# Where single-token state space steps, a gate's last products and the layer's input are placed in a hybrid layer

## The chip, the cores and the metric

One core of a Trainium2 chip runs the whole kernel. The metric is the device time of one execution in microseconds (us); a version is run several times and the median is shown. Inputs and outputs are float32 arrays in the chip's memory.

## The reference

One layer of a decoder is computed for 1024 prompt tokens and for 8 single tokens ("samples", one per sequence, each with a state of its own from earlier). Cut to what matters here:

```python
proj = rmsnorm(x, norm1_w) @ w_in                 # q, f, i, g, z, xbc, dt
xbc = silu(causal_dwconv(xbc, buf, conv_w, b))    # x (16 heads of 64), B and C (2 groups of 128)
# state space group: for a sample token, one step
S_new = exp(A * dt) * S + (x * dt) outer B
y = S_new @ C + D * x
y = rmsnorm(y * silu(z)) per group of 512 channels
# HGRN2 group: 8 heads with a matrix state, own gate and norm
x = x + concat([o_hgrn, y]) @ w_out               # the layer's input x is added here
x = x + (silu(conv(gate)) * val) @ w_down         # gate, val = rmsnorm(x) @ w_up
y = rmsnorm(x) * final_w
```

For the prompt tokens the state space part is computed in 8 chunks of 128 tokens. All new states are outputs too.

## The kernel before

The activations are kept with channels on the 128 partitions and tokens along the free dimension: 1032 columns, 1024 of the prompt (`T`) and 8 of the samples (`T:NT`). Every large product is made of three matmuls on rounded parts (high by high, high by low, low by high), so the tensor engine has much to do.

The work before `w_down` is a list of **jobs**, each with one weight tile. A job of the input projection is 72 matmuls (three column blocks of 344). The order is x0 to x3 (first group's x), x9 and x11 (second group's B and C), x4 to x7 (second group's x), z0 to z3 (first gate), the first head's f, q, v, sg, then z4 to z7, then the other heads' jobs f1 to sg7. The first group's B and C tiles (j = 8 and 10) are made ahead of the list. Then come the jobs of the output projection `o{r0}.{m}`: o8.0, o8.2, o12.0, o12.2, o8.4, o8.6, o12.4, o12.6, and then o0 and o4 in two halves; rows 8 to 15 are the state space part, 0 to 7 the heads. A job of o8 sets two tiles of the sum (`A.copy`, L1038), the later ones add to them (L1040).

A **stream** runs beside jobs: `drive(stream, weight, name)` issues a stretch of the stream and then so many matmuls of jobs in proportion. `ssd(0)` (first group, 8 chunks) runs beside x9 to x7, `ssd(1)` beside z0 to the first head's q, and `head(h)` beside later jobs; `head(7)`, the last, runs beside o8.0 to o12.2. `ssd_front` builds a chunk's decays (`csb`, L530, L531, L546) and transposes x (`xp`, L541); `ssd_back` makes its output and the next state (`yo`, `st`, `yd`, L563 to L582).

`tick()` is called at each job matmul; `after(n, work)` runs `work` n ticks later, and `spread(pieces, n)` runs a generator one piece at a time, n ticks apart. Code that is issued earlier has priority. Only the tensor engine keeps the written order (`manual_schedule`). For the other engines and the DMA queue on SP the framework's scheduler makes an order when the program is built: an instruction that it holds to be ready may come ahead of earlier code. That order is then fixed, and each queue runs in it and waits at its head. `fetch` ties a load behind the last weight load issued (`issue_after`).

**The parts that the change touches:**
- `decode_bc(g)` (L606) transposes the samples' columns of B and C, copies them (`bcr`, L611) and writes them to memory (`bc_d`, L612). It is the first thing in the stream `ssd(g)`, so for group 0 it stands behind x3.
- `ssm_decode(g, i)` (L614) is the single step of x tile i for all 8 samples, in two halves of four. A half loads `Bb`, `Cb` and the state `Sd` (L623 to L626), scales the state on ScalarE (L627, four instructions), forms the new state on VectorE (L628, L629), stores it (L630), multiplies it by C on GpSimd (L631) and sums on VectorE (L632). The result goes into the samples' columns of the x tile (L633). `ddb` (dt and decay) is loaded at L499. Buffers: four for `Bb` and `Cb` together (tag `d`), two for `Sd` (tag `ld`). For group 0 the steps are issued at the start of x5, x7, z0 and z1; for group 1 at z4 to z7.
- `tail()` in `ssm_gate(g)` (L679) makes the four normalized products of a group (L683, 128x1032 each) and stores them (L684), all four where the norm of the last column block is ready, some 36 (group 0) or 50 (group 1) ticks into the job behind the gate.
- `residual_load(m)` (L756) loads 128 columns of the layer's input into two `xs` tiles (tag `d` as well) and an `xd`; `residual` transposes them (L774, L778) and adds them to the sum (L769), in two pieces 8 ticks apart. It is done for tiles m and m+1 in each of the four jobs of o8. `mix_load(r0)` loads four tiles of the mixers' output for the jobs of `r0` and splits them into high (ScalarE, L998) and low parts (VectorE, L999).

```python
    with tc.manual_schedule(engines={mybir.EngineType.PE}):
        finish("x3")
        drive(ssd(0), 45.5, "x7")
        drive(ssd(1), 45.5, "v0")
        finish("z7")
        for h in range(H):
            drive(head(h, heads[h]), 32.0 if h else 35.0, f"sg{h + 1}" if h < H - 1 else "o12.2")
        finish("o12.6")
```

Of the kernel before, what the change touches and what calls it, by code (L numbers as in the profile page):

```python
# [12 lines left out]
ALU = mybir.AluOpType  # L13
# [37 lines left out]
def hybrid_layer(  # L51
# [9 lines left out]
    V, A, G, PE, SP = nc.vector, nc.scalar, nc.gpsimd, nc.tensor, nc.sync  # L61
# [9 lines left out]
    def nm(s):  # L71
        cnt[0] += 1
        return f"{s}_{cnt[0]}"
# [142 lines left out]
    def after(n, work):  # L216

        later.append([n, work])
# [8 lines left out]
    def spread(pieces, n, then=None):  # L227

        def go():
            if next(pieces, 0) is None:  # L230
                after(n, go)
            elif then is not None:
                then()
        go()
# [115 lines left out]
    def xbc_close(j, ext):  # L350
# [6 lines left out]
        A.activation(acc[:, T:NT], acc[:, T + 3:T + 32:4], AF.Silu)  # L357
        return acc

    def xbc_job(j, put):  # L360
        ext = []
        def begin():
            ext.append(xbc_open())
            if j in (5, 7):
                ssm_decode(0, (5, 7).index(j))

        in_job(f"x{j}", OFF_X + j * P, lambda c, cs, ps: xbc_evict(j, ext[0], c, cs, ps), begin=begin, end=lambda: put(xbc_close(j, ext[0])))

# [65 lines left out]
    d_bc = const.tile([P, 8], F32, name="d_bc")  # L434
# [165 lines left out]
    def d4(t):  # L600
        return t.rearrange("p (b n) -> p b n", n=P)
# [4 lines left out]
    def decode_bc(g):  # L606
        bcps = bank("bc", "nx")
        for i, src in enumerate((BT[g], CT[g])):
            PE.transpose(bcps[:ND, i * P:(i + 1) * P], src[:, T:NT], ident)
        bcr = small.tile([ND, 2 * P], F32, tag="bcr", bufs=1, name=nm("bcr"))  # L610
        V.tensor_copy(bcr, bcps[:ND, :2 * P])  # L611
        SP.dma_start(bc_d[2 * g:2 * g + 2].rearrange("i b n -> b i n"), bcr.rearrange("b (i n) -> b i n", n=P))  # L612

    def ssm_decode(g, i):  # L614
        j = g * 4 + i
        xdd = small.tile([P, 2, ND], F32, tag="xdd", name=nm("xdd"))
        xdec = Xg[g][i][:, T:NT]
        V.tensor_tensor(xdd[:, 0, :], xdec, ddb[:, 0, j, :], op=ALU.mult)
        for b0 in (0, 4):
            bs = slice(b0, b0 + 4)  # L620
            Bb, Cb = tl("d", "Bb")[:, :512], tl("d", "Cb")[:, :512]
            for t_, r in ((Bb, 2 * g), (Cb, 2 * g + 1)):
                fetch(t_, bc_d[r, bs].rearrange("b n -> (b n)").unsqueeze(0).to_broadcast([P, 512]))  # L623
            Sd = tl("ld", "Sd")
            fetch(d4(Sd), state_ssm[0, bs, 2 * j:2 * j + 2].rearrange("b h p n -> (h p) b n"))
            for b in range(4):  # L626
                A.activation(d4(Sd)[:, b, :], d4(Sd)[:, b, :], AF.Copy, scale=ddb[:, 1, j, b0 + b:b0 + b + 1])  # L627
            V.tensor_tensor(d4(Bb), d4(Bb), cb(xdd[:, 0, bs]), op=ALU.mult)  # L628
            V.tensor_tensor(Sd, Sd, Bb, op=ALU.add)  # L629
            SP.dma_start(ssm_sample[0, bs, 2 * j:2 * j + 2].rearrange("b h p n -> (h p) b n"), d4(Sd))  # L630
            G.tensor_tensor(Cb, Sd, Cb, op=ALU.mult)  # L631
            V.tensor_reduce(xdd[:, 1, bs], d4(Cb), axis=mybir.AxisListType.X, op=ALU.add)  # L632
        V.scalar_tensor_tensor(xdec, xdec, d_bc[:, j:j + 1], xdd[:, 1, :], op0=ALU.mult, op1=ALU.add)  # L633

    def rstd_of(dst, tmp, ps, n):

# [5 lines left out]
    def ssm_gate(g):  # L642
        acc = []

        def z_job(i):
            j = g * 4 + i

            def begin():
                if i == 0:
                    acc.append(tl("g", "gacc"))  # L650
                if g:
                    ssm_decode(1, i)
                elif i < 2:
                    ssm_decode(0, i + 2)

            def evict(c, cs, ps):
                Y = Xg[g][i][:, cs]
                sz = tl("z", "sz")[:, :CH]
                A.activation(sz, ps, AF.Silu)
                V.tensor_tensor(Y, Y, sz, op=ALU.mult)  # L660
                if i == 0:
                    A.activation(acc[0][:, cs], Y, AF.Square)
                else:
                    A.activation(sz, Y, AF.Square)
                    (V if g or i == 3 else G).tensor_tensor(acc[0][:, cs], acc[0][:, cs], sz, op=ALU.add)
                if i == 3:
                    after(36 + 14 * g, lambda: rstd(c))
            in_job(f"z{j}", OFF_Z + j * P, evict, begin=begin)

        def rstd(c):  # L670
            cs = chunks[c]
            ps = bank("ms", "nx")
            mm(ps[:, :CH], ones, acc[0][:, cs])
            rstd_of(acc[0][:, cs], tl("z", "nt")[:, :CH], ps[:, :CH], 512)

            if c == NCH - 1:
                tail()

        def tail():  # L679
            for i in range(4):  # L680
                j = g * 4 + i
                Y = Xg[g][i][:, :NT]
                V.scalar_tensor_tensor(Y, Y, col("sn", j), acc[0][:, :NT], op0=ALU.mult, op1=ALU.mult)  # L683
                SP.dma_start(mix_d[8 + j], Y)  # L684

        for i in range(4):
            z_job(i)
# [13 lines left out]

    def ssd(g):
        parts = {}
        decode_bc(g)
        yield 6.5
        ssd_front(g, 0, parts)
        for c in range(1, NC):
            yield 2.5
            ssd_front(g, c, parts)
            yield 2.5  # L710
            ssd_back(parts, c - 1)
        yield 3.0
        ssd_back(parts, NC - 1)
        yield 1.0
        ssm_state_out(g)
# [40 lines left out]
    def residual_load(m):  # L756
        ms = slice(m * P, (m + 1) * P)
        xs = [tl("d", "xs")[:, :512] for _ in range(2)]
        xd = small.tile([ND, P], F32, tag="xd", name=nm("xd"))
        for i in range(2):  # L760
            fetch(xs[i].rearrange("p (i m) -> p i m", m=P),
                  x_prompt[0, i * 512:(i + 1) * 512, ms].rearrange("(i p) m -> p i m", p=P))
        fetch(xd, x_sample[:, 0, ms])
        return xs, xd
# [20 lines left out]
    xh = [[None] * KT for _ in range(2)]  # L785
# [226 lines left out]
    x1_d = dram.tile([KT, P, NT], F32, name="x1_d")  # L1012
    rst = tl("g", "n2r")

    def out_job(r0, m, halves=(0, 1), last=False):
        def load():
            w = wload(w_out[0, r0 * P:(r0 + 4) * P, m * P:(m + 2) * P], 4, 2 * P)
            return w, [residual_load(m + i) for i in range(2)] if r0 == 8 else None

        def run(loads):  # L1020
            w, res = loads
            if r0 not in mixes:
                mixes[r0] = mix_load(r0)
            hi, lo = mixes[r0]
            if res:
                for hf in range(2):
                    xpair[hf][m // 2] = tl("big", "x1")[:, :NT].rearrange("p (i t) -> p i t", i=2)
                    for i in range(2):
                        xh[hf][m + i] = xpair[hf][m // 2][:, i, :]
            for i in range(2):  # L1030
                for hf in halves:
                    for c in range(2):
                        cs, ts_ = slice(c * QW, (c + 1) * QW), slice((2 * hf + c) * QW, (2 * hf + c + 1) * QW)
                        ps = psmm.tile([P, 512], F32, tag="mm", name=nm("mm"))[:, :QW]
                        yield from steps(w, i * P, (i + 1) * P, hi, lo, ts_, ps)
                        x_ = xh[hf][m + i][:, cs]
                        if res:
                            A.copy(x_, ps)  # L1038
                        else:
                            V.tensor_tensor(x_, x_, ps, op=ALU.add)  # L1040
                        if last:
                            final(m + i, x_, ts_)
                        yield True
                if res:
                    spread(residual([xh[hf][m + i] for hf in range(2)], *res[i]), 8)
        job(f"o{r0}.{m}" + (f".{halves[0]}" if len(halves) == 1 else ""), load, run)

    def final(m, x_, ts_):
# [30 lines left out]
    for hf in range(2):  # L1079
        for r0 in (0, 4):  # L1080
            for m in range(0, KT, 2):
                out_job(r0, m, (hf,), r0 == 4)

    with tc.manual_schedule(engines={mybir.EngineType.PE}):
        finish("x3")
        drive(ssd(0), 45.5, "x7")
# [5 lines that stand above are left out]
        for r0 in (0, 4):  # L1092
            mixes[r0] = mix_load(r0)
# [307 lines left out]
    for c in (3, 0, 1, 2):  # L1401
# [4 lines left out]
        for t0 in range(cs.start, cs.stop, P):  # L1406
# [11 lines left out]
            for i in range(2):  # L1418
# [4 lines left out]
                else:  # L1423
                    V.scalar_tensor_tensor(ot[i][:n], tb[i][:n, :], ss[:n, 3:4], fw[:n, ds],  # L1424
                                           op0=ALU.mult, op1=ALU.mult)
# [31 lines left out]
```

## Time and profile before

| | |
|---|---|
| median of 3 runs | 1781.82 us (1781.15 to 1788.02) |
| the profiled execution's own time | 1782.61 us |
| its span, first to last instruction | 1780.9 us |
| TensorE matmul busy | 1725.4 us, 97% of the span |
| VectorE, ScalarE, GpSimd busy | 63%, 46%, 23% |
| DMA | 182.34 MB, mean 102 GB/s |

PE is the tensor engine, DVE is VectorE, ACT is ScalarE, POOL is GpSimd, SP the engine whose queue issues nearly all DMAs. A row of instructions has line, engine, operation, output and inputs. "Idle before" is the time in which the engine stood still ahead of an instruction, with what ended that. In a table of waits the three numbers are the sum in us, how often, and the longest. A granted clock of 1.00 is 2.4 GHz on the tensor engine, 0.50 is 1.2 GHz.

### The profile page before, as it was taken

The numbers are of one execution on the slowest core, as the hardware profiler recorded it, in microseconds if no ns is written. First come the engines' busy times: TensorE is split into PE (matmuls) and PEld (weight loads), VectorE is DVE, ScalarE is ACT, GpSimd is POOL, SyncE is SP. The second block draws the span as 40 slices with busy tenths as digits, with TensorE's granted clock in tenths as the row PEclk, the third lists the DMA queues.
The fourth block names the chain that finished last, engine by engine and source line by source line (L and its number), as shares of the span: only waits on it lengthen the run. The fifth ranks groups of instructions, "written<-read, shape, count | busy, mean of one in ns | idle before, by whom it ended". The sixth has DMA issues, their size and how long they took to land. (4 is left out here: it accounts for less than half of the span.)

```text
span 1780.9 us, 38506 instructions
## 1 busy us (share of the span) xinstructions
PE 1725.4 (97%) x16143; PEld 1675.6 (94%) x16143; DVE 1119.3 (63%) x2011; ACT 817.5 (46%) x1464; POOL 405.3 (23%) x415
## 2 busy tenths in 40 slices
PE   7999899999999999999999978999999999999998
PEld 6998799999999999999899978999999999999997
DVE  6667966575564565458645768666666666445545
ACT  7677688455554454545333435334333344111114
POOL 2113331220110111011000364554445542000001
PEclk9999999999999999999999998999999999999999
DMA  4144634642221222234334432222222225422212
GB/s 154 39 126 126 189 106 132 184 137 98 87 66 51 86 73 78 58 109 155 101 108 133 135 90 72 72 72 78 82 91 72 72 84 203 152 81 90 97 61 96
DMA packets 218019, 182.34 MB, mean 102 GB/s; under 512 B 13388, under 2 KB 195158, under 8 KB 217830
## 3 DMA queue, kind: packets, MB, share of 16 engines
q1 hardware_dynamic: 217558, 179.80, 32.3%
q8 instruction: 126, 2.06, 0.5%
q14 instruction: 47, 0.39, 0.1%
q0 software_dynamic: 288, 0.10, 0.0%
HBM read 141.53 MB, written 38.52 MB: 101 GB/s over the span
## 5 line engine op out<-in xcount | busy, mean ns | idle before, releaser
L93 PE MATMUL mm<-hh,wh 128*128 128x344 f32 x1248 | 405.3, 325 | 0.3 <-issue 0.2
L93 PE MATMUL mm<-hl,wh 128*128 128x344 f32 x1248 | 404.5, 324 | 0.0
L93 PE MATMUL mm<-hh,wl 128*128 128x344 f32 x1248 | 402.0, 322 | 0.0
L93 PEld LDWEIGHTS mm<-hh,wh 128*128 128x128 f32 x1248 | 235.0, 189 | 3.9 <-issue 2.6
L93 PEld LDWEIGHTS mm<-hl,wh 128*128 128x128 f32 x1248 | 235.2, 189 | 2.4 <-issue 0.9
L93 PEld LDWEIGHTS mm<-hh,wl 128*128 128x128 f32 x1248 | 235.3, 189 | 2.2 <-issue 1.5
L183 ACT CAST wh<-ws 128x1024 fp32r<-128x1024 f32 x96 | 100.5, 1047 | 242.8 <-PE dn L93 135.3
L93 PE MATMUL ub<-ul,wh 128*128 128x258 f32 x704 | 200.4, 285 | 4.3 <-DVE ul L1144 4.3
L93 PE MATMUL ub<-uh,wh 128*128 128x258 f32 x704 | 200.3, 285 | 2.0 <-ACT uh L1143 2.0
L93 PE MATMUL ub<-uh,wl 128*128 128x258 f32 x704 | 200.2, 284 | 0.0
L93 PE MATMUL dn<-ah,wh 128*128 128x256 f32 (+1 forms) x640 | 181.1, 283 | 1.2 <-DVE x L1387 1.2
L93 PE MATMUL dn<-al,wh 128*128 128x256 f32 (+1 forms) x640 | 180.6, 282 | 0.0
L93 PE MATMUL dn<-ah,wl 128*128 128x256 f32 (+1 forms) x640 | 180.2, 282 | 0.0
L184 DVE TENSOR_TENSOR wl<-ws,wh 128x1024 fp32r<-128x1024 f32 x96 | 126.4, 1317 | 72.4 <-ACT wh L183 71.4
L93 PE MATMUL mm<-mh,wh 128*128 128x258 f32 x512 | 147.7, 288 | 11.2 <-DVE x L1040 8.3
L93 PE MATMUL ua<-ul,wh 128*128 128x258 f32 x528 | 149.4, 283 | 0.9 <-DVE ul L1144 0.9
L93 PE MATMUL ua<-uh,wh 128*128 128x258 f32 x528 | 149.2, 283 | 0.0
L93 PE MATMUL ua<-uh,wl 128*128 128x258 f32 x528 | 148.4, 281 | 0.0
L93 PE MATMUL mm<-ml,wh 128*128 128x258 f32 x512 | 145.8, 285 | 0.7 <-DVE ml L999 0.7
L93 PE MATMUL mm<-mh,wl 128*128 128x258 f32 x512 | 145.9, 285 | 0.0
L93 PEld LDWEIGHTS ub<-ul,wh 128*128 128x128 f32 x704 | 134.5, 191 | 5.0 <-DVE ul L1144 5.0
L93 PEld LDWEIGHTS ub<-uh,wh 128*128 128x128 f32 x704 | 134.0, 190 | 2.5 <-ACT uh L1143 2.5
(347 smaller groups left out, 3942.8 us busy)
## 6 DMA issues: line engine op xcount, KB each, us to landing
ws<-in_w_in_dram SPq DMA_DIRECT2D x52, 512.0 KB
ws<-in_w_up_dram SPq DMA_DIRECT2D x44, 512.0 KB
ws<-in_w_out_dram SPq DMA_DIRECT2D x24, 512.0 KB
act_d<-val SPq DMA_DIRECT2D x22, 516.0 KB
al<-act_d SPq DMA_DIRECT2D x22, 516.0 KB
ws<-in_w_down_dram SPq DMA_DIRECT2D x22, 512.0 KB
ml<-mix_d SPq DMA_DIRECT2D x48, 172.0 KB
csb<-cs_d SPq DMA_DIRECT2D x32, 256.0 KB
```

Of the source, the lines that this page charges most:

```text
L93: PE.matmul(out, lhsT, rhs, start=start, stop=stop)
L183: A.copy(wh[:, :n], ws[:, :n])
L184: V.tensor_tensor(wl[:, :n], ws[:, :n], wh[:, :n].bitcast(F32), op=ALU.subtract)
```

## The change

`decode_bc(0)` is issued ahead of the job list, where B and C of group 0 are ready. Group 0's four single steps are issued at the start of x2, x3, x9 and x11. In all eight steps the sums L632 and the result L633 are issued 36 ticks after the rest of the step (`outputs`). The gate's four products are issued 10 ticks apart. The layer's input is loaded and added in o8.4, o8.6, o12.4 and o12.6 (tiles 0 to 1, 2 to 3, 4 to 5, 6 to 7) and no longer in o8.0 to o8.6.

```diff
+    DEC0 = (2, 3, 9, 11)
     def xbc_job(j, put):
...
-            if j in (5, 7):
-                ssm_decode(0, (5, 7).index(j))
+            if j in DEC0:
+                ssm_decode(0, DEC0.index(j))
...
             G.tensor_tensor(Cb, Sd, Cb, op=ALU.mult)
-            V.tensor_reduce(xdd[:, 1, bs], d4(Cb), axis=mybir.AxisListType.X, op=ALU.add)
-        V.scalar_tensor_tensor(xdec, xdec, d_bc[:, j:j + 1], xdd[:, 1, :], op0=ALU.mult, op1=ALU.add)
+            Cs.append(Cb)
+        def outputs():
+            for i, Cb in enumerate(Cs):
+                V.tensor_reduce(xdd[:, 1, 4 * i:4 * i + 4], d4(Cb), axis=mybir.AxisListType.X, op=ALU.add)
+            V.scalar_tensor_tensor(xdec, xdec, d_bc[:, j:j + 1], xdd[:, 1, :], op0=ALU.mult, op1=ALU.add)
+        after(36, outputs)
...
                 if g:
                     ssm_decode(1, i)
-                elif i < 2:
-                    ssm_decode(0, i + 2)
...
             if c == NCH - 1:
-                tail()
+                spread(tail(), 10)
...
                 SP.dma_start(mix_d[8 + j], Y)
+                yield
...
     def ssd(g):
         parts = {}
-        decode_bc(g)
+        if g:
+            decode_bc(g)
...
+    RES = {(8, 4): 0, (8, 6): 2, (12, 4): 4, (12, 6): 6}
...
-            return w, [residual_load(m + i) for i in range(2)] if r0 == 8 else None
+            return w, [residual_load(RES[r0, m] + i) for i in range(2)] if (r0, m) in RES else None
...
-            if res:
+            if r0 == 8:
...
-                        if res:
+                        if r0 == 8:
                             A.copy(x_, ps)
...
-                    spread(residual([xh[hf][m + i] for hf in range(2)], *res[i]), 8)
+                    spread(residual([xh[hf][RES[r0, m] + i] for hf in range(2)], *res[i]), 8)
...
+    decode_bc(0)
     with tc.manual_schedule(engines={mybir.EngineType.PE}):
         finish("x3")
```

## Rows read from the trace of the kernel before

**Rows 1.** The page, part 1: busy us, share of the span, instructions of an engine.
```profile
PE 1725.4 (97%) x16143; PEld 1675.6 (94%) x16143; DVE 1119.3 (63%) x2011; ACT 817.5 (46%) x1464; POOL 405.3 (23%) x415
```

**Rows 2.** PE's waits, 150 to 230 us.
```profile
PE xp L541 <- DVE ecs L563: 3.0, 2, 2.2
PE yo L93 <- DVE S L569: 2.6, 1, 2.6
PE xp L541 <- ACT xbc L356: 1.2, 1, 1.2
PE yd L93 <- DVE xdt L543: 0.8, 1, 0.8
PE sT L594 <- DVE S L569: 0.6, 1, 0.6
```

**Rows 3.** PE's waits, 400 to 416 us, and 815 to 896 us.
```profile
PE a L93 <- DVE q L854: 2.5, 1, 2.5
...
PE mm L93 <- ACT x L1038: 2.8, 1, 2.8
PE a L93 <- DVE v L854: 0.7, 1, 0.7
...
PE xtd L778 <- DVE odr L924: 0.4, 1, 0.4
```

**Rows 4.** Windows: length, busy (count) by PE, PEld, DVE, ACT, POOL, PE clock, DMA.
```profile
196.00:214.00 18.00, 13.93 (x93) 10.97 (x92) 17.67 (x27) 8.84 (x21) 7.06 (x5) 0.91 0.61 158
400.00:416.00 16.00, 13.35 (x317) 12.70 (x316) 14.03 (x20) 9.61 (x13) 0.00 (x0) 0.89 0.45 167
844.00:858.00 14.00, 10.81 (x121) 9.79 (x120) 9.76 (x21) 7.14 (x18) 0.00 (x0) 0.88 0.59 174
```

**Rows 5.** Groups of instructions, 94 to 230 us: the single steps of group 0.
```profile
L631 POOL TENSOR_TENSOR Cb<-Sd,Cb 128x512 f32<-128x512 f32 x8 | 11.6, 1453 | 19.6 <-DVE Sd L629 14.8 <-DMA Cb<-bc_d 4.9
L627 ACT ACTIVATE Sd<-Sd,ddb 128x128 f32<-128x128 f32 x32 | 10.7, 395 | 10.6 <-DMA Sd<-in_state_ssm_dram 10.6
L629 DVE TENSOR_TENSOR Sd<-Sd,Bb 128x512 f32<-128x512 f32 x8 | 6.3, 802 | 0.0
L628 DVE TENSOR_TENSOR Bb<-Bb,xdd 128x512 f32<-128x512 f32 x8 | 6.3, 790 | 0.3 <-DMA Bb<-bc_d 0.3
L632 DVE TENSOR_REDUCE xdd<-Cb 128x4 f32<-128x512 f32 x8 | 5.4, 680 | 5.1 <-POOL Cb L631 5.1
```

**Rows 6.** The same table of windows: four stretches of the first group's chunks.
```profile
94.00:116.00 22.00, 22.00 (x143) 21.89 (x142) 11.30 (x15) 18.35 (x30) 0.49 (x4) 1.00 0.35 99
116.00:150.00 34.00, 34.00 (x245) 31.15 (x244) 27.18 (x44) 27.59 (x61) 7.36 (x9) 1.00 0.43 125
150.00:176.00 26.00, 23.82 (x170) 21.74 (x169) 19.55 (x36) 18.03 (x37) 9.81 (x10) 1.00 0.57 162
176.00:214.00 38.00, 32.95 (x224) 28.54 (x222) 36.49 (x59) 23.83 (x55) 14.10 (x12) 0.96 0.66 186
```

**Rows 7.** Timeline of DVE, 95 to 98 us.
```profile
97.07 0.28 DVE L618 TENSOR_TENSOR xdd<-xbc,ddb 128x8 f32<-128x8 f32 x2 [3.52 <-DMA ddb<-dd_d]
```

**Rows 8.** The waits of the DMA queue on SP, 94 to 230 us.
```profile
SPq L175 <- PE yo L93: 7.5, 1, 7.5
```

**Rows 9.** Timeline of DVE, 380 to 425 us: the second gate's products.
```profile
403.15 4.90 DVE L683 SCALAR_TENSOR_TENSOR xbc<-xbc,vcol,gacc 128x1032 f32<-128x1032 f32 x4
```

**Rows 10.** ACT's waits, 815 to 870 us.
```profile
ACT mh L998 <- DMA ml<-mix_d: 7.7, 5, 3.5
```

**Rows 11.** Timeline of the DMA queue on SP, 828 to 850 us.
```profile
838.68 0.45 SPq L175 DMA_DIRECT2D xs<-in_x_prompt_dram  x1
...
846.06 1.70 SPq L175 DMA_DIRECT2D ml<-mix_d  x2
```

**Rows 12.** Groups of instructions, 815 to 870 us: the additions of the layer's input.
```profile
L769 DVE TENSOR_TENSOR x<-x,xtp 128x512 f32<-128x512 f32 (+2 forms) x12 | 5.8, 504 | 6.7 <-PE xtp L774 6.7
```

**Rows 13.** The table of windows for o12.4 and o12.6.
```profile
924.00:948.00 24.00, 24.00 (x200) 23.79 (x200) 14.29 (x34) 8.00 (x15) 0.00 (x0) 1.00 0.45 143
```

More of the change, by code (lines that the diff above doesn't have):

```diff
@@ L617, in ssm_decode @@
         xdec = Xg[g][i][:, T:NT]
+        Cs = []
         V.tensor_tensor(xdd[:, 0, :], xdec, ddb[:, 0, j, :], op=ALU.mult)
```

## The prediction

> **What bounds the kernel.** I read the page's busy times first: the tensor engine is busy for 97% of the span and VectorE for 63% [rows 1]. No change here takes matmuls away or adds any: the transposes of B, C and of the layer's input only move. So the sum can only be made of time in which the tensor engine stands still, and of time in which it runs at the lower of its two clocks. The second view is therefore its table of waits, cut to the stages that the change touches. Between 150 and 230 us, beside the first group's chunks, it waits 3.0 + 2.6 + 1.2 + 0.8 + 0.6 = 8.2 us, nearly all of it for VectorE [rows 2]. Beside the first heads it waits 2.5 us in one piece, and beside the last head, where the output projection begins, 2.8 + 0.7 + 0.4 = 3.9 us [rows 3] (shorter ones aside).
>
> The third view is the windows around the three longest of these waits. The mean granted clock there is 0.91 over 18 us, 0.89 over 16 us and 0.88 over 14 us [rows 4]. Each time the clock falls to 1.2 GHz for a few us right behind the wait of 2.5 to 2.8 us. It costs what it lacks to full speed: 18 x 0.09 = 1.6, 16 x 0.11 = 1.8, 14 x 0.12 = 1.7 us. The wait of 2.2 us [rows 2] is no such case: from 150 to 176 us, where the engine stands still for 26 - 23.82 = 2.2 us, the clock is 1.00 [rows 6]. So all that the three stages have to give is 8.2 + 1.6, 2.5 + 1.8 and 3.9 + 1.7 us, 19.7 us together, or 1.1%.
>
> **Part 1: the single steps of group 0.** Nothing of the work goes away. Four steps are 18.0 us of VectorE (6.3 + 6.3 + 5.4, two small operations a step left out), 10.7 us of ScalarE and 11.6 us of GpSimd [rows 5]. What matters is beside what they run. Now they crowd the late chunks: from 176 to 214 us VectorE is busy for 36.5 of 38 us, 96%, and that is where most of the waits lie [rows 6, 2]. Earlier there is room: 22 - 11.3 = 10.7 us from 94 to 116 us and 34 - 27.2 = 6.8 us from 116 to 150 us [rows 6].
>
> The new place in the code lies before that, at x2 and x3. But the scheduler already pulls these instructions ahead: the first operation of two steps, written at x5 and at x7, ran as a pair at 97.07 us, where it had waited 3.52 us for `ddb` [rows 7]. `ddb` does not move. So the steps cannot start before some 97 us; what the change can do is to let all four run from there, one behind the other through the four `d` buffers, instead of having B and C ready only in the stream. I count 17.5 us of room against 18.0 us of work, and some 2.7 us of that work is in the second stretch already (two each of L628 and L629 by their means [rows 5]). So it fits by 150 us only if VectorE is never idle, which no in-order queue manages; I expect the last step to end at some 165 us. ScalarE is as tight: it has 22 - 18.35 + 34 - 27.59 = 10.1 us there for 10.7 us [rows 6, 5].
>
> So the late waits should go: the 8.2 us and the 1.6 us of clock, 9.8 us. In their place come waits in chunks 1 to 4, where VectorE and ScalarE now come near 100%. Nothing of before shows that load there. The nearest row is the stretch with 96%, whose waits are 4.8 us of the 8.2 (2.6 + 0.8 + 0.6 and what the 3.0 has beside its 2.2 [rows 2]); the bounds are 0 and the whole 8.2 us. I take 3.5 us, below that row, since conv work of x9 to x7 can be put off there and the sums can too: VectorE stood still for 5.1 us before L632, waiting for GpSimd [rows 5], and 36 ticks later the product will be there. **Part 1: -9.8 + 3.5 = -6.3 us**, between -9.8 and the +1.8 of rival 2.
>
> The transposes of B and C for `bc_d` go to the start of x0, into the tensor engine's queue, where a late SiLU could hold them. Before, this stretch has no wait; between 0 and 1.2 us (the wait for a SiLU [rows 2]) I take 0. Queue SP issues as many DMAs as before, eight a step, 50 us earlier. For group 1 the later sums hold `Cb` for up to half a job more; its steps run in a stretch without a wait of the tensor engine, so 0.
>
> **Part 2: the gate's products.** The second gate's four run in one piece of 4.90 us from 403.15 us [rows 9]; behind them in VectorE's queue stands the head's scaling, whose operand q ends the 2.5 us wait [rows 3]. One product at a time does not mean one between each pair of other operations. The norm of the third block is issued some 30 ticks ahead of that scaling, so products 1 to 3 (at 0, 10 and 20 ticks) keep their priority, and since they all wait for the same norm they will still run in one piece. The fourth, at 30 ticks, falls behind. That takes 4.90 / 4 = 1.2 us out of the chain. What is left is a wait of 1.3 us, shorter than the 2.2 us behind which the clock stayed [rows 6], so the 1.8 us go too. **Part 2: -1.2 - 1.8 = -3.0 us**, between 0 and -4.3. The first gate's products stand in a stretch without such a wait: 0.
>
> **Part 3: the layer's input.** Beside the last head, VectorE loses the twelve additions of four tiles, 5.8 us [rows 12], and queue SP loses their loads. The second is worth more. The 2.8 us wait is for ScalarE, which has to copy a sum out of PSUM; it was held in its queue by rounding `ml` tiles that had not come, 7.7 us in five waits [rows 10]. They had not come since SP issued `xs` loads, waiting for `d` buffers, between them; the last `ml` left at 846 us, and `xs` had its turn from 838 us on [rows 11]. Without them I expect the `ml` loads some 8 us sooner, and that wait gone. With VectorE's 5.8 us the 0.7 us for v and the 0.4 us go as well. So 3.9 us and the clock's 1.7 us. What comes in place: two tiles in o12.4 and two in o12.6, 5.8 us on a VectorE that is busy for 14.29 of 24 us there [rows 13]: covered, 20 of 24. The last half tile falls into o0.0, at the next split. I take 0.5 us for it, between 0 and 3.0. **Part 3: -5.6 + 0.5 = -5.1 us**, between -5.6 and -2.6.
>
> **The sum.** -6.3 - 3.0 - 5.1 = -14.4 us on the profiled execution's 1782.6 us gives 1768.2 us; the median of the runs is 0.8 us less, which I leave aside: **1768 us**.
>
> **Rivals.**
> 1. *All goes.* No new waits, no remainder: -9.8 - 4.3 - 5.6 = -19.7, **1763 us**. For it: the conv work has slack. Against it: the 17.5 us of room.
> 2. *The crowd only moves.* VectorE and ScalarE are full in chunks 1 to 4 and part 1 gives nothing: 1782.6 - 8.1 = **1774.5 us**. For it: the room equals the work. GpSimd can add to that. If each of the eight L631 products holds VectorE for its 1453 ns [rows 5], the work grows by 11.6 us beyond the room, and with 9.8 us won the stage ends 1.8 us slower: 1782.6 + 1.8 - 8.1 = 1776.3 us. The Trainium skill, "SBUF — State Buffer", section "Who interferes with whom", has such a rule: a VectorE operation with two SBUF inputs and a GpSimd operation that reads SBUF lock each other out. By that rule, which speaks against a denser stretch, the 1776.3 us would hold. The trace agrees only in part: L629, with two SBUF inputs, takes 802 ns in the mean [rows 5], so a lock of 1453 ns can have met few of them.
> 3. *It does not do what it says.* The scheduler's order, not the place in the code, decides [rows 7]. The four products stay in one piece and two of the four steps stay late: half of part 1 and part 3, -3.2 - 5.1, **1774 us**.
> 4. *Slower: SP blocks.* The loads of step 2, 3 and 4 need `d` buffers that the step before gives back only after its sums, 36 ticks on. If the order has them ahead of the chunks' `csb` loads and the weights, SP waits at its head; its longest such wait now is 7.5 us [rows 8]. It decides from the point where a wait is longer than the chunk's lead, about half a job. Three such waits in full, 22.5 us, with nothing won in part 1: 1782.6 + 22.5 - 8.1 = **1797 us**. Against it: that 7.5 us wait now costs the tensor engine nothing, since nothing waits before 150 us [rows 6].
>
> **How the numbers follow.** A measurement of this kernel tells 0.5% from no change, 8.9 us: below 1772.9 us is faster, above 1790.7 us slower. The forecast has 0.45, rival 1 0.13, rival 2 0.18, rival 3 0.14, rival 4 0.10. Of the forecast 0.03 lies above 1772.9 us. So faster 0.55, same 0.35, slower 0.10. The range 1760 to 1782 holds all but rival 4 and the ends of the others.
>
> **What would show it.** Right: single steps between 97 and 165 us; VectorE well below 96% from 176 to 214 us and no wait over 2 us there; three products together and the fourth behind the scaling near 408 us; no `xs` load between the `ml` loads of o12, and no fall of the clock near 206, 411 and 851 us. Wrong: new waits of 8 us before 165 us; SP at rest for over 8 us ahead of `csb`; waits in o12.4 to o0.0.

## The result, and the profile after

The changed kernel takes 1793.51 us (median of 7 runs, 1790.87 to 1795.6) against 1783.93 us (7 runs of the kernel before on the same chip): a ratio of 1.0047 over all runs, 95% interval 1.0033 to 1.0062, or 5.9 to 11.1 us more (the medians differ by 9.6 us). It is slower, by half a percent. The profiled execution took 1795.6 us, the longest of the seven; its span is 1793.8 us, 12.9 us above that of before.

The busy times do not show that. Page, part 1, of the changed kernel, against [rows 1]:

```profile
PE 1729.7 (96%) x16143; PEld 1681.6 (94%) x16143; DVE 1115.4 (62%) x2011; ACT 817.5 (46%) x1464; POOL 411.9 (23%) x415
```

So I cut both traces into stages, from the first matmul of one job to that of another (x4 starts at 133.37 us and x0 at 58.26 us before, which makes 75.1 us). The last stage runs from the end of sg7 to the first matmul of o0.4, so it holds o8.0 to o12.6, o0.0 and o0.2. The third row holds all traces of this study in which that stage's own code is that of before; it shows how far a stage scatters. (Run 9, which leaves the steps out, is not in it: there x0 to x4 takes 76.4 us.)

| us | x0 to x4 | x4 to z1 | z1 to f1 | f1 to v1 | end of sg7 to o0.4 |
|---|---|---|---|---|---|
| before | 75.1 | 94.1 | 158.5 | 32.3 | 136.8 |
| changed | 90.3 | 84.5 | 160.7 | 33.2 | 140.4 |
| stage's code as before | 75.1 to 75.2 | 94.1 to 95.7 | 158.5 to 161.8 | 32.3 to 34.0 | 135.3 to 138.5 |

Three stages lie outside the scatter: +15.2 us where the steps went, -9.6 us where they came from, and about +2.5 us at the output projection (medians of 139.8 and 137.3 us over the traces with the layer's input moved and not moved). They make +8.1 us, against 8.4 us by the ratio.

**Where the steps came from.** PE's waits from 94 to 230 us in the changed kernel, against [rows 2], which stood between 150 and 230 us (none stood ahead of that):

```profile
PE xp L544 <- ACT xbc L356: 6.8, 1, 6.8
PE mm L93 <- DVE last L348: 4.2, 1, 4.2
PE yo L93 <- DVE S L572: 1.5, 1, 1.5
```

and the windows, against [rows 6]:

```profile
94.00:116.00 22.00, 17.77 (x104) 17.52 (x103) 11.19 (x19) 14.25 (x33) 5.90 (x5) 0.92 0.73 199
116.00:150.00 34.00, 27.17 (x170) 25.95 (x170) 28.85 (x45) 27.46 (x59) 14.12 (x13) 0.90 0.74 206
150.00:176.00 26.00, 26.00 (x193) 23.17 (x192) 20.71 (x35) 20.18 (x42) 8.28 (x8) 1.00 0.36 102
176.00:214.00 38.00, 38.00 (x269) 34.90 (x268) 29.42 (x50) 25.46 (x53) 9.06 (x11) 1.00 0.37 103
```

From 150 to 214 us the tensor engine now never stands still, and VectorE fell from 96% to 77% in the last of the four windows. From 94 to 150 us there are two waits, 4.2 and 6.8 us, and the clock is at 0.92 and 0.90: 22 x 0.08 + 34 x 0.10 = 5.2 us more. Together 16.2 us, for the 15.2 us of the table. Yet VectorE is not full there: 40.0 of 56 us, 38.5 before.

**The 4.2 us.** Timeline of ACT, then of DVE, in the changed kernel:

```profile
94.57 0.20 ACT L357 ACTIVATE xbc<-xbc 128x8 f32<-128x8 f32 x1
101.27 2.45 ACT L631 ACTIVATE Sd<-Sd,ddb 128x128 f32<-128x128 f32 x8 [6.51 <-DMA ddb<-dd_d]
103.63 0.41 ACT L344 COPY ext<-mm 128x336 f32<-128x336 f32 x1
```
```profile
97.33 0.17 DVE L622 TENSOR_TENSOR xdd<-xbc,ddb 128x8 f32<-128x8 f32 x1 [3.76 <-DMA ddb<-dd_d]
101.81 0.69 DVE L632 TENSOR_TENSOR Bb<-Bb,xdd 128x512 f32<-128x512 f32 x1 [4.31 <-DMA Bb<-bc_d]
...
106.33 0.16 DVE L348 COPY last<-mm 128x11 f32<-128x11 f32 x1
```

ScalarE's next instruction in its order was the scaling of a state, which needs the decays in `ddb`. By the trace these had landed at 101.27 us (the part of `ddb` with dt, which VectorE reads, at 97.33 us); behind the scaling stood the copy of x2's last PSUM bank (L344), which takes 0.41 us and whose matmuls had ended at 94.85 us. VectorE stood for 3.76 us as in [rows 7] and then 4.31 us more for `Bb`; x2's two small copies out of PSUM stood behind six operations of the first two steps and came at 106 us. The tensor engine needed that bank, and the last to free it was VectorE: ScalarE's copy was done at 104.0 us, VectorE's at 106.5 us, and the matmuls went on at 106.64 us.

**The 6.8 us.** PE transposes the first chunk's x when x3's SiLU is done. Timelines of ACT, of the kernel before and of the changed one:

```profile
114.51 1.06 ACT L356 ACTIVATE xbc<-xbc 128x1024 f32<-128x1024 f32 x1 [0.52 <-DVE xbc L334]
115.47 0.20 ACT L357 ACTIVATE xbc<-xbc 128x8 f32<-128x8 f32 x1
```
```profile
122.11 1.28 ACT L631 ACTIVATE Sd<-Sd,ddb 128x128 f32<-128x128 f32 x4 [3.35 <-DMA Sd<-in_state_ssm_dram]
...
128.20 1.06 ACT L356 ACTIVATE xbc<-xbc 128x1024 f32<-128x1024 f32 x1
```

and of DVE in the changed kernel, the last operation of x3's convolution:

```profile
122.97 1.31 DVE L334 SCALAR_TENSOR_TENSOR xbc<-ext,vcol,xbc 128x1056 f32<-128x1056 f32 x1
```

Before, the SiLU ended at 115.6 us and the transposes began at 116.21 us: half a microsecond of slack. Now x3's matmuls ended 6.0 us later (112.20 against 106.20 us), by the first wait and the slow clock behind it. VectorE had the second step's last sum and result between the operations of x3's convolution, which ended at 124.3 us. ScalarE waited 3.35 us for the third step's state ahead of the SiLU, which came at 128.20 us, 3.9 us behind the convolution.

**The gate's tail.** DVE, against [rows 9]:

```profile
410.74 3.69 DVE L691 SCALAR_TENSOR_TENSOR xbc<-xbc,vcol,gacc 128x1032 f32<-128x1032 f32 x3
414.35 0.69 DVE L803 TENSOR_SCALAR k<-f 128x1032 f32<-128x1032 f32 x1
414.96 1.22 DVE L184 TENSOR_TENSOR wl<-ws,wh 128x1024 fp32r<-128x1024 f32 x1
416.09 1.29 DVE L691 SCALAR_TENSOR_TENSOR xbc<-xbc,vcol,gacc 128x1032 f32<-128x1032 f32 x1
417.30 0.69 DVE L863 TENSOR_TENSOR f<-f,tt 128x512 f32<-128x512 f32 x1
417.90 0.69 DVE L864 TENSOR_TENSOR q<-q,tt 128x512 f32<-128x512 f32 x1
```

The fourth product is out of the piece, but still ahead of the head's scaling. The wait for q is 2.5 us, as in [rows 3].

**The output projection.** PE's longest waits from 822 to 902 us, and SP's timeline, against [rows 3, 11] (o8.0 starts at 829.90 us, 822.16 us before), with two lines of SP of before and two of ACT of the changed kernel:

```profile
PE mm L93 <- ACT x L1051: 4.7, 2, 3.5
...
```
```profile
839.43 0.39 SPq L846 DMA_DIRECT2D out_dram<-Sh  x1
839.92 0.46 SPq L175 DMA_DIRECT2D ml<-mix_d  x1
842.58 0.38 SPq L846 DMA_DIRECT2D out_dram<-Sh  x1
843.01 6.91 SPq L175 DMA_DIRECT2D ml<-mix_d  x11
```
```profile
833.68 1.38 SPq L175 DMA_DIRECT2D ml<-mix_d  x3
...
838.19 0.39 SPq L836 DMA_DIRECT2D out_dram<-Sh  x1
```
```profile
847.64 2.32 ACT L1008 CAST mh<-ml 128x344 fp32r<-128x344 f32 x5 [4.58 <-DMA ml<-mix_d]
...
851.24 0.37 ACT L1051 COPY x<-mm 128x258 f32<-128x258 f32 x1
```

The `xs` loads are gone, but now all twelve `ml` loads stand behind the first of the two stores of the last head's states, and eleven behind both; the stores wait for GpSimd, 4.7 us in two waits. Before, seven of the twelve had left SP ahead of the stores. The last `ml` left 20.0 us behind the first matmul of o8.0 (849.92 - 829.90), 25.6 us before; the first one 10.0 us behind it, 7.0 us before. ScalarE stood for 4.58 us for one of them, and the copy out of PSUM that ended the 3.5 us wait stood behind that.

### The profile page after: what moved, and what is told of

Read it like the earlier page. It is cut to its first block, busy times and chain, and to the rows that moved or that the text cites. A ratio compares the mean times of both kernels' runs of the same rounds, so it can differ in the third digit from the quotient of the medians.

```text
span 1793.8 us, 38499 instructions
## 1 busy us (share of the span) xinstructions
PE 1729.7 (96%) x16143; PEld 1681.6 (94%) x16143; DVE 1115.4 (62%) x2011; ACT 817.5 (46%) x1464; POOL 411.9 (23%) x415
## 3 DMA queue, kind: packets, MB, share of 16 engines
q1 hardware_dynamic: 217558, 179.80, 32.3%
## 4 chain that ended last, share of the span: by engine, by line
PE 47%; DVE 3%; DMA 1%; issue 1%; ACT 1%; POOL 0%; SPq 0%; DVEq 0%; POOLq 0%; ACTq 0%
PE ub L93 14%; PE dn L93 14%; PE ua L93 10%; PE mm L93 8%; DMA ml<-mix_d 1%; DVE x L1147 0%; PE fin L1426 0%; POOL wt L1222 0%; DVE wl L1242 0%; PE xtp L784 0%; DVE ul L1158 0%; DMA ws<-in_w_up_dram 0%; DVE wl L184 0%; DVE x L1053 0%; PE o L93 0%
## 5 line engine op out<-in xcount | busy, mean ns | idle before, releaser
L93 PEld LDWEIGHTS ub<-uh,wh 128*128 128x128 f32 x704 | 134.5, 191 | 2.6 <-ACT uh L1157 2.5
```

Source lines behind the costliest of these rows:

```text
L93: PE.matmul(out, lhsT, rhs, start=start, stop=stop)
```

## The experiments

Ratios are to the kernel before on the same chip (medians of 1784.7 to 1788.4 us from chip to chip), with 95% intervals.

**1. The steps alone** (sums in place).

```diff
+    DEC0 = (2, 3, 9, 11)
...
-            if j in (5, 7): ...
+            if j in DEC0: ...
...
-                elif i < 2: ...
...
-        decode_bc(g)
+        if g: ...
...
+    decode_bc(0)
```

> The kernel before with one part of the change: group 0's steps at x2, x3, x9 and x11 and its B and C transposed ahead of the list; sums in place, gate tail and layer input as before. Theory A (the early crowd costs more than the late one gave): x2 and x3 are held by ScalarE standing at the head of its queue for ddb and by the second step ahead of x3's convolution; about 15 us are lost by the end of x9 and 9 to 10 us won back in the chunks, so some +5 us, 1787 to 1791 us. Rival B (the early waits come from the deferred sums, which hold the d buffers longer): with the sums in place the early loss is below 5 us and the run is faster than before, 1776 to 1780 us.

1.0034 (1.0022 to 1.0047), +6.1 us. x0 to x4 is 89.2 us, x4 to z1 88.0 us. PE's waits, 94 to 230 us:

```profile
PE xp L543 <- ACT xbc L356: 6.1, 1, 6.1
PE mm L93 <- DVE last L348: 3.5, 1, 3.5
...
```

Theory A by the difference (the kernel before takes 1788.11 us on this chip): the later sums are not the cause. From x4 to z1 it wins 6.1 us and not theory A's 9 to 10: the changed kernel, with the later sums, wins 9.6 us there.

**2. The layer's input alone.**

```diff
+    RES = {(8, 4): 0, (8, 6): 2, (12, 4): 4, (12, 6): 6}
...
```

> The kernel before with the layer input moved alone: loaded and added in o8.4, o8.6, o12.4 and o12.6. Theory A (the ml loads stand behind the stores of the last states Sh, not behind the xs loads; the transposes and additions only move): no gain at o12.0, one new wait at o12.6 and the later clock, +2 to +5 us against before. Rival B (the ml loads were late in the changed kernel only since all of it was 8 us later and in another order): the move alone gives what was forecast for it, -3 to -5 us.

1.0012 (1.0000 to 1.0024), +2.1 us. From the end of sg7 to o0.4 it takes 140.35 us, as in the changed kernel: up to o8.4 it is 70.8 us (71.9 to 75.6 us with the input unmoved, median 74.2), from there to o0.4 69.6 us (62.8 to 63.4 us, median 63.1). Against the medians 3.4 us left the first part and 6.5 us came up in the second. Over 4 us of each are the tensor engine's 36 transposes of four tiles (4.3 us in the trace of before, from one start to the next), which stand in the second part now: without them the first part won nothing. Theory A, at the low end of its range.

**3. The sums and the tail alone.**

```diff
+        after(36, outputs)
...
-                tail()
+                spread(tail(), 10)
```

> The kernel before with the sums of the single steps issued 36 ticks later and the gate's products issued 10 ticks apart, and nothing else. Theory A (neither is worth anything: the fourth product still comes ahead of the head's scaling, and the sums were covered): within 2.5 us of before, with the 2.5 us wait for q near 405 us and the slow clock behind it still there, and some 1 to 2 us lost beside z5 to f1. Rival B (the later sums hold the d buffers and so the steps of both groups): +4 us or more by z7.

1.0001 (0.9991 to 1.0010). The 2.5 us wait for q is there. Theory A. The three parts make 6.1 + 2.1 + 0.2 = 8.4 us, as the whole change does (1783.93 x 0.0047).

**4. The steps from x9 on.**

```diff
-    DEC0 = (2, 3, 9, 11)
+    DEC0 = (9, 11, 4, 5)
```

> The changed kernel with one line changed: the steps of group 0 issued at x9, x11, x4 and x5 in place of x2, x3, x9 and x11. Theory A (the place, ahead of x3's convolution and beside the ddb load, is what costs): the waits of 4.2 us near 102 us and 6.8 us near 122 us and the slow clock behind them (15 us together) go for the most part, and the late chunks keep the better part of their relief (VectorE below 96 percent): 9 to 14 us under the changed kernel, 1780 to 1784 us. Rival B (the crowd only moves: the work of four steps has no room before 150 us wherever it starts): the loss shows up in chunks 1 to 5 in other waits, and the run is within 4 us of the changed kernel, 1790 us or more.

1.0006 (0.9993 to 1.0019): about 7 us under the changed kernel, between the two theories. The wait beside x2 is down to 0.6 us, but not the one for x3's SiLU:

```profile
PE xp L544 <- ACT xbc L356: 5.4, 1, 5.4
PE yd L93 <- DVE xdt L546: 2.7, 1, 2.7
...
```

The trace suggests why: written at x9, the first step's `Bb` load still left SP at 92.43 us, beside x2, since B and C were in memory by then. Run 5 tests that.

**5. B and C written behind x3 again**, on the kernel of run 4.

```diff
-    decode_bc(0)
...
-        if g:
-            decode_bc(g)
+        decode_bc(g)
```

> The changed kernel with the steps of group 0 at x9, x11, x4 and x5 and with the transposes of B and C for memory back at the head of the stream, behind x3, as before the change. Theory A (with B and C in memory early, the order pulls the first step's loads and operations into x2 and x3, wherever the step is written; the head of VectorE's and ScalarE's queues then waits there): the 5.4 us wait of the first chunk's transposes near 117 us and the slow clock behind it go, and the late relief stays: 6 to 9 us under the run with the steps at x9, 1.003 to 1.005 below the kernel before on the same chip. Rival B (the work of the steps is too much for 94 to 150 us, whatever its order): another wait of 4 us or more comes up before 165 us and the time is within 3 us of the run with the steps at x9.

1.0022 (1.0012 to 1.0032). The first chunk's 5.4 us wait is gone and x0 to x4 is down to 79.5 us, as theory A had it, but x4 to z1 rises to 91.1 us. PE's waits, 94 to 230 us:

```profile
PE yd L93 <- DVE bt L541: 3.8, 2, 2.3
PE xp L544 <- DVE xdt L546: 2.7, 1, 2.7
PE xp L544 <- DVE S L572: 1.1, 1, 1.1
PE yo L93 <- DVE S L572: 1.0, 1, 1.0
```

Rival B: x0 to z1 is 170.6 us here and with the steps from x9 (169.2 to 170.9 us in the traces with that code as before, 174.8 us changed). Freed of the two waits of the changed kernel, the steps still cost what they cost late.

**6. The tail behind the scaling**, on the kernel before.

```diff
-                tail()
+                after(36, lambda: spread(tail(), 10))
```

> The kernel before with the gate's four products issued 10 ticks apart from 36 ticks after the norm on, so that three of the four stand behind the head's scaling in VectorE's order. Theory A (the 4.90 us of products in that queue are what the wait for q is made of): the 2.5 us wait near 405 us and the slow clock behind it go, 3 to 4.5 us under before. Rival B (the scaling waits for something else too, a norm or a weight's low part, so the products only fill idle time): the wait stays above 1.5 us and the time is within 2 us of before.

0.9989 (0.9977 to 1.0000), -2.0 us; f1 to v1 is 28.5 us, 3.8 us under before. DVE's timeline, and the window with the clock at 1.00:

```profile
405.12 1.28 DVE L683 SCALAR_TENSOR_TENSOR xbc<-xbc,vcol,gacc 128x1032 f32<-128x1032 f32 x1
...
408.66 0.68 DVE L855 TENSOR_TENSOR q<-q,tt 128x512 f32<-128x512 f32 x1
...
410.80 3.69 DVE L683 SCALAR_TENSOR_TENSOR xbc<-xbc,vcol,gacc 128x1032 f32<-128x1032 f32 x3
```
```profile
395.00:425.00 30.00, 30.00 (x596) 28.50 (x596) 24.57 (x36) 17.84 (x27) 3.84 (x3) 1.00 0.44 141
```

Theory A for the stage. The time of the whole shows half of it; its interval, 0 to 4.1 us less, holds the 3.8 us and ends at nothing.

**7 and 8. `ml` of o12 earlier**, on the changed kernel and on the one before.

```diff
+            if (r0, m) == (8, 2):
+                mixes[12] = mix_load(12)
```

> The changed kernel with the second four ml tiles (for o12) loaded and split at the start of o8.2 in place of o12.0; six of their twelve loads then stand ahead of the two Sh stores on queue SP, all twelve behind them in the changed kernel. Theory A (the sum in PSUM waits for ScalarE, ScalarE for ml, and ml for the Sh stores): the 3.5 us wait near 848 us falls to under 1.5 us and the slow clock of 6.8 us behind it is halved or gone, 3 to 6 us under the changed kernel. Rival B (ScalarE or VectorE are simply full there with the splits and the last head): the wait only moves to o8.2, within 2 us of the changed kernel.

> The kernel before with the same one edit: the second four ml tiles loaded and split at the start of o8.2, so that all twelve loads stand ahead of the Sh stores and of the xs loads of o8.2. The layer's input stays where it was. Theory A (the late ml loads, not the additions of the layer's input, make the 2.8 us wait for a PSUM copy): that wait and the slow clock behind it go, 3 to 5 us under before, with the layer's input unmoved. Rival B (VectorE's additions are the load): the wait stays above 2 us, within 2 us of before.

On the changed kernel 1.0037 (1.0024 to 1.0050); end of sg7 to o0.4 falls by 3.5 us to 136.9 us, and the 3.5 us wait to 0.3 us (of 2.0 us in two). On the one before 0.9991 (0.9978 to 1.0005); the stage takes 134.5 us, 0.8 us under the lowest of the unmoved. The 2.8 us wait of [rows 3] is gone from its place, with the slow clock behind it; one of 1.6 us stands 36 matmuls ahead of that place:

```profile
PE mm L93 <- ACT x L1040: 1.6, 1, 1.6
...
```

Theory A for the wait on the changed kernel, and for the better part of it on the one before, where theory A had it gone; the intervals do not tell either time from that of the kernel it was made from. Late `ml` loads make most of that wait, with the layer's input in either place.

**9. Without group 0's steps.**

```diff
-            if j in (5, 7): ...
...
-                elif i < 2:
-                    ssm_decode(0, i + 2)
```

> The kernel before with the four single steps of group 0 left out (their states and their samples' outputs are not computed). This is the floor: what the four steps cost at all in the stage of the first group's chunks, wherever they stand. Theory A (18 us of VectorE and 11 us of ScalarE have no room in 94 to 214 us, so any place there costs about what the late one does): 8 to 10 us under before, no wait of the tensor engine above 1.5 us from 116 to 230 us. Rival B (the chunks themselves, not the steps, make the late waits): within 4 us of before, with waits for S and ecs still there.

0.9921 (0.9906 to 0.9936), -14.1 us; x0 to z1 is 159.2 us, 10.0 us under before, with one wait of 1.0 us. Theory A for the stage: about that is all that any place can win in it. By its interval the whole shows 1 to 7 us more than the stage; where they lie is left open.

**10 and 11. The steps later**, the last two at z2 and z3, or all four at z0 to z3.

```diff
-                elif i < 2:
-                    ssm_decode(0, i + 2)
+                elif i >= 2:
+                    ssm_decode(0, i)
```

That is run 10's edit; run 11 takes the steps out of x5 and x7 too, and the z jobs call `ssm_decode(g, i)`.

> The kernel before with the last two of group 0's steps issued later instead of earlier: the third at z2 and the fourth at z3 (z0 and z1 before). Theory A (the crowd is a matter of VectorE's load, and behind 228 us it has room: 28.6 of 46 us busy from 228 to 274 us): the waits for S between 196 and 216 us and the slow clock at 206 us go, no new wait above 1 us up to 275 us, 4 to 7 us under before. Rival B (the single steps delay the gate's products of z2 and z3 or ScalarE, 85 percent busy there, and PE waits for its PSUM banks): new waits from 228 to 275 us and a time within 2 us of before or above.

> The kernel before with all four steps of group 0 issued later: step i at z job i, so that nearly nothing of them is left beside the first group's chunks. Theory A: nearly the floor, 6 to 10 us under before, VectorE below 85 percent from 150 to 214 us. Rival B (the four now follow one another in 190 to 270 us and the first two come too late for z0's and z1's third block, since VectorE's queue then waits for their loads at its head): waits of 3 us or more between 214 and 245 us, and no more than 2 us under before.

0.9985 (0.9975 to 0.9995) and 0.9971 (0.9960 to 0.9982). x0 to z1 is 163.2 and 161.7 us, close to the floor, and z1 to f1 163.4 and 166.3 us, above the scatter. PE's longest wait with all four, 94 to 275 us:

```profile
PE ms L93 <- DVE gacc L660: 3.3, 1, 3.3
...
```

The fourth step, ahead of it in VectorE's order, makes the sum for z3's norm late. At 2.7 and 5.2 us both gains lie below their theories' 4 to 7 and 6 to 10 us, though the intervals reach into these. With all four, the new wait at z3 and the slow clock behind it take back some 5 us; z0 and z1 have no wait above 0.2 us. With the last two that wait is 1.5 us, and a wait of 2.0 us for `vd` near 382 us with slow clock behind it takes back more; what makes that one is left open.

**12. Together:** the steps at z0 to z3, that norm 60 ticks behind its block (the edit moves the second gate's norm too, from 50 to 60), the tail of 6 and the `ml` loads of 8. Its diff, without what 6 and 8 show:

```diff
-            if j in (5, 7): ...
...
-                if g:
-                    ssm_decode(1, i)
-                elif i < 2:
-                    ssm_decode(0, i + 2)
+                ssm_decode(g, i)
...
-                    after(36 + 14 * g, lambda: rstd(c))
+                    after(60, lambda: rstd(c))
```

> A version built from what the runs showed, on the kernel before: all four steps of group 0 at z0 to z3, the norm of the first gate 60 ticks behind its last block in place of 36 (its sum came 3.3 us late with the steps at z0 to z3), the gate's products 10 ticks apart from 36 ticks after the norm, and the second ml tiles at the start of o8.2. Theory A (the three effects stand in different stages and add up): 5 us for the steps, 2 for the products, 2 for ml and up to 3 for the norm, so 9 to 12 us under before, a ratio of 0.993 to 0.995. Rival B (later products and norms hold tiles and PSUM banks that the first heads need): the gains stay under 5 us, the ratio is above 0.997.

1776.75 us (5 runs) against 1784.7 us (9 runs), 0.9955 (0.9942 to 0.9969), -8.0 us: below both kernels, 1 us short of theory A. x0 to z1 161.4 us, f1 to v1 30.8 us (28.5 us in run 6), end of sg7 to o0.4 134.5 us; z1 to f1 is still 163.2 us, with a 2.4 us wait for the norm:

```profile
PE ms L93 <- DVE nt L636: 2.4, 1, 2.4
...
```

## Why the prediction was wrong

**Part 1, what it removes: right.** -9.8 us forecast, -9.6 us in x4 to z1. VectorE is below 96% there, the waits for ecs and S are gone but for 1.5 us, and no fall of the clock is left at 206 us. Run 1 shows that some 3.5 of these 9.6 us hang on the later sums, to which the forecast gave no part of its own.

**Part 1, what comes in place: the step that failed.** "Nothing of before shows that load there. The nearest row is the stretch with 96%": I priced new waits by how full VectorE would be, 3.5 us, at most 8.2 us. They cost 15.2 us on a VectorE that was busy for 71% of the stretch, and the last step's sum ran at 146 us, where the text expected 165. They were not made by load, but by what stood at the head of two queues, and by how little slack lay behind. The text had both signs and used neither. It had VectorE waiting 3.52 us for `ddb` [rows 7], and drew from it only that the steps start at 97 us; but ScalarE's scaling needs `ddb` too [rows 5], and whatever PSUM copy stands behind it in that order waits with it; on VectorE the copies stood behind `Bb` in the same way. And it took a stretch without a wait [rows 6] for room, where x3's SiLU was half a microsecond ahead of its use. Runs 4 and 5 show this part by part: with the steps from x9 the x2 wait goes, with B and C in memory only behind x3 the SiLU's wait goes. Whether one of the two queues alone would have made the x2 wait was not run. (A slip beside this: by the means of [rows 5], two each of L628 and L629 are 3.2 us and not 2.7; the forecast does not hang on it.)

**Rival 2, that the crowd only moves, holds beneath that.** Runs 4 and 5 end at x0 to z1 of 170.6 us, no better than late: of the changed kernel's 174.8 us the order of the queues makes 4.2 us, and the rest of what was won late is lost early in other waits. Its GpSimd variant does not hold for the changed kernel. Groups of instructions, 94 to 230 us, changed kernel, against [rows 5]:

```profile
L635 POOL TENSOR_TENSOR Cb<-Sd,Cb 128x512 f32<-128x512 f32 x8 | 14.0, 1744 | 18.6 <-DVE Sd L633 17.0 <-DVE ext L346 1.4
L633 DVE TENSOR_TENSOR Sd<-Sd,Bb 128x512 f32<-128x512 f32 x8 | 5.5, 685 | 0.1
```

GpSimd's product got longer (1453 to 1744 ns), but VectorE's two-input sum got shorter (802 to 685 ns). By the lock of two-input VectorE operations and GpSimd reads that the Trainium skill names in "SBUF — State Buffer", section "Who interferes with whom", the order of issue decides which side is blocked; in this trace only GpSimd's side got longer. With the steps from x9 (run 4) both did, to 1935 and 930 ns. What made them longer is not shown.

**Part 2: the order was wrong, the mechanism right.** "The fourth, at 30 ticks, falls behind": it did not; k, a weight's low part and then the fourth product went ahead of the scaling, and so the whole 4.9 us stayed there and -3.0 us became nothing. Run 6, where three do fall behind, wins 3.8 us in the stage, within the 0 to -4.3 us of that part.

**Part 3: the wrong blocker.** "They had not come since SP issued `xs` loads": with these gone the Sh stores held the `ml` loads, and the wait rose from 2.8 to 4.7 us in two. -5.1 us became about +2.5 us. What comes in place was sized too low, within its bounds: the additions are covered in o12.4 and o12.6, where no wait stands, but in o0.0 and o0.2 two new waits for the sums make 1.6 us, for a forecast of 0.5. The tensor engine's own transposes only moved. PE's waits of the changed kernel, 902 to 975 us:

```profile
PE mm L93 <- DVE x L1053: 1.6, 2, 0.8
```

**Rival 4** gave 1797 us, near what came, but not by its mechanism: no wait of the tensor engine there is for `csb` or a weight. Its idea, that a wait at the head of a queue decides, held on ScalarE and VectorE instead of SP.

## What to carry to other kernels

Before work is moved into a stretch without waits, ask two things of the trace: how much slack the next consumer has there (the end of its last producer against its own start), and what lands last among the moved work's inputs, on every engine that reads it; a short copy queued behind it will wait as long. An engine's idle share prices neither. Work with a late deadline (the steps are needed only in the gate) was better moved towards that deadline here (runs 10 to 12) than away from it, and what decides between two instructions is the engine's final order, which is to be read after each edit.

## What the runs showed of the hardware that was not expected

- The clock did not follow the length of a wait alone. Waits of 2.0 us were followed by a fall in the run with the last two steps at z2 and z3 near 382 us, and not near 154 us; the 4.2 us wait of the changed kernel was followed by some 3 us at 1.2 GHz, the 6.8 us wait by some 7 us. So the one wait of 2.2 us behind which the clock stayed [rows 6] did not allow the inference of part 2 that a shorter one costs no clock.
- Stages whose code is untouched differ by over 3 us from one kernel's trace to another's (z1 to f1: 158.5 to 161.8 us in three traces), where x0 to x4 agrees within 0.1 us. An offset of two traces is therefore to be read inside a stage.
